# A mixture-of-experts decoder layer: the low halves of x1 made by VectorE, its scaling folded into a later addition, and the router stage in another order

## The chip, the cores and the metric

The kernel runs on one core of a Trainium2 chip. The metric is the device time of one execution in microseconds. A core has five engines, each with its own in-order instruction queue: TensorE (PE; PEld is its weight load), VectorE (DVE), ScalarE (ACT), GpSimd (POOL) and SyncE (SP), which here only starts transfers. An instruction waits on semaphores for results of other engines, and everything behind it in the same queue waits too.

## What is computed

One decoder layer on 512 tokens of 1024 numbers, all in float32. Two mixers work on a common projection of x: four mLSTM heads and eight attention heads with a sliding window. Then:

```python
y = concat(mlstm_out, att_out) @ w_out          # 512x1024 @ 1024x1024
x = layer_norm(ALPHA * x + y, ln1_w, ln1_b)     # "x1" in the kernel
# router: best of 4 groups, then the best 2 of that group's 8 experts
g_idx = argmax(x @ w_group_router + b_group_router)
top_v, top_i = top_k((x @ w_expert_router + b_expert_router)[group g_idx], 2)
out = sum over the 32 experts e of combine[:, e] * (silu(x @ w_gate[e]) * (x @ w_up[e])) @ w_down[e]
x = layer_norm(ALPHA * x + out, ln2_w, ln2_b)
```

An expert has three matrices of 1 MB, so the weights of the 32 experts are 96 MB.

## The kernel before, in words

The tokens are cut into four chunks of 128 rows; chunk c of x1 is one tile of 128x1024 (in the order listings the four tiles are x_2218, x_2221, x_2224 and x_2227, for chunks 0 to 3). The program has three parts.

The first part (up to about 200 us) is the projection and the two mixers. The second is the **router stage**, which the change rewrites. It is written out by hand: the order of the calls in the source is the order of the instructions on PE, DVE, ACT and POOL. For each chunk it has these steps:

- `out_mm`, `ml_late` (helper lines 194 to 196): the output projection on PE into the PSUM tiles `py`; three matmuls per product, since each operand is split in a high and a low half.
- `norm_a` (L864 to L867, then L199 and L200 on POOL): ALPHA * x + y and its statistics on DVE, then the reciprocal root on POOL.
- `norm_b` (L876, L877 on DVE; or L880 on POOL, L881 on ACT, L882 and L883): scale and shift, by halves of 512 columns. The table `NB` says which engine does which half. For chunk 2 it is DVE for half 0, and ACT and POOL for half 1; for chunk 3 it is DVE for both.
- `route_t`, `route_m` (L911, L912, L922): x1 is transposed on PE, copied from PSUM by ACT (`x1T`), and multiplied with the router's weights on PE into `lg`.
- `rd` (L931 to L954): the best group and the best two experts, some nine small instructions on DVE, ending in the one-hot tile `ohs` (L950). `rr` (L979 to L992): each token's rank inside its expert, by one to four small matmuls on `ohs` and five small DVE instructions, ending in `cola`.
- `x1_hi`, `x1_lo` (L895, L899): ACT makes a rounded copy `x1h` of x1 and another engine makes `x1l` = x1 - x1h. Both write column q*8+j of x1 to place (j, q), so x1 is read with a step of eight numbers, 32 bytes, and the copies are written in a row.
- `first_hot` (L1000, L1002): a one-hot matrix from `cola`, on DVE. `first_pick` (L1007): PE multiplies it with `x1h` and `x1l`, which gathers the tokens of the first two pairs of experts into four PSUM tiles `xp`. Per chunk these are 16 matmuls, four for each tile. A tile is complete when all four chunks are in it, and ACT then copies it (L1015).

When the last pick is done, the first pass through expert weights starts (`gu_part`, L1094). DVE meanwhile works out which expert takes which place (`slots_a`, L1198 to L1219), and PE and DVE turn that into the table `eid` (L1225).

The third part goes through 13 pairs of experts. SP loads weights in the order of use into a ring of buffers: seven of 8 KB per partition from the start, two more from another pool, five when the projection's weights are done with, four when `ml_late` is. The first six experts have fixed places and are loaded before the router is done; all others need `eid`, from which SP reads the expert's number, and a buffer that a pass has set free. Near the end `y_gather` (L1150, L1152) fetches each token's two expert results with eight gathers and adds them to x1 on DVE. Before that, x1 is multiplied by ALPHA, on POOL, right after the router stage (L1508).

Of the kernel before, what the change touches and what calls it, by code (L numbers as in the profile page):

```python
# [17 lines left out]
OP = mybir.AluOpType  # L18
# [5 lines left out]
NCH = 4  # L24
# [11 lines left out]
ALPHA = 2.0 ** 0.25  # L36
# [43 lines left out]
def layer_kernel(ctx, tc, x, w_in, conv_w, conv_b, gate_bias, norm_w, sinks, w_out, ln1_w, ln1_b,  # L80
# [17 lines left out]
    def close_pool(key):  # L98
        pools.pop(key)[0].__exit__(None, None, None)
# [7 lines left out]
    def open_ring(key, n, side):  # L107
        open_pool(key, n, 2 * DM, side)
        free.extend([key] * n)
# [514 lines left out]
    def prefetch(n):  # L624
        while loads and free and n > 0:
            p, i, b = loads.pop(0)
            if free[0] == "mix":
                key, ts = free.pop(0), [slot("we")[:, :DM] for _ in range(2)]
            else:
                t, key = rslot("we", n=2 * DM)  # L630
                ts = [t]
            assert key != "mix" or i == 2
            KEYS[p][i == 2].append(key)
            pairs[p][b][i] = load_part(ts, expert(SEATS[p][b]), i)
            n -= 1
# [234 lines left out]
    def norm_b(c, h):  # L870
        xc_ = x1[c]
        mv = n1[c][1]
        hs = slice(h * 512, (h + 1) * 512)
        xh_ = xc_[:, hs]
        if NB[c][h] == "V":
            V.scalar_tensor_tensor(xh_, xh_, mv[:, 0:1], l1w[:, hs], op0=OP.subtract, op1=OP.mult)  # L876
            V.scalar_tensor_tensor(xh_, xh_, mv[:, 2:3], l1b[:, hs], op0=OP.mult, op1=OP.add)  # L877
        else:
            if h == 0 or NB[c][0] == "V":
                G.tensor_scalar(mv[:, 3:4], mv[:, 2:3], mv[:, 0:1], -1.0, op0=OP.mult, op1=OP.mult)  # L880
            A.activation(xh_, xh_, AF.Identity, bias=mv[:, 3:4], scale=mv[:, 2:3])  # L881
            (V if NB[c][h] == "M" else G).tensor_mul(xh_, xh_, l1w[:, hs])  # L882
            G.tensor_add(xh_, xh_, l1b[:, hs])  # L883
# [9 lines left out]
    def x1_hi(c, halves=None):  # L893
        for hi, _, v in x1_parts(c, halves):
            A.activation(hi, v, AF.Copy)  # L895

    def x1_lo(c, halves=None, eng=G):
        for hi, lo, v in x1_parts(c, halves):
            eng.tensor_tensor(lo, v, hi, op=OP.subtract)  # L899

# [245 lines left out]
    def y_gather():  # L1146
        for c in range(NCH):
            for k in range(2):
                t = slot("yg")[:, :DM]
                G.indirect_dma_start(out=t, out_offset=None, in_=yd[:, :],  # L1150
                                     in_offset=bass.IndirectOffsetOnAxis(ap=yrow[:, 2 * c + k:2 * c + k + 1], axis=0))
                V.tensor_add(x1[c], x1[c], t)  # L1152

    def y_slots():
        return [slot(n, F32R)[:, :DM] for n in ("yh", "yl")]
# [205 lines left out]
    def rd(c, n):  # L1361
        if c not in gd:
            gd[c] = route_d(c)
        some(gd[c], n)
# [6 lines left out]
    with tc.manual_schedule(engines=MAN):  # L1371
        out_mm(0, 0, (0,), (0, 1))
        out_mm(0, 0, (1,), (0, 1))
        out_mm(0, 0, (0,), (2, 3))
        out_mm(0, 0, (1,), (2, 3))
        norm_a(0, (0,))
        norm_a(0, (1,))
        norm_b(0, 0)
        out_mm(1, 0, (0,), (0, 1))
        out_mm(1, 0, (1,), (0, 1))  # L1380
        out_mm(3, 1, (0,), (0, 1))
        norm_b(0, 1)
        out_mm(1, 0, (0,), (2, 3))
        out_mm(1, 0, (1,), (2, 3))
        route_t(0, (0,))
        out_mm(3, 1, (1,), (0, 1))
        route_m(0, (0,))
        route_t(0, (1,))
        out_mm(3, 1, (0,), (2, 3))
        route_m(0, (1,))  # L1390
        out_mm(2, 0, (0,), (0, 1))
        norm_a(1, (0,))
        norm_a(1, (1,))
        norm_b(1, 0)
        out_mm(3, 1, (1,), (2, 3))
        rd(0, 4)
        norm_b(1, 1)
        rd(0, 4)
        rd(0, 9)
        rr(0, 1)  # L1400
        x1_hi(0)
        route_t(1, (0,))
        x1_hi(1)
        close_pool("wr"); open_ring("ring1", NR // 2, "left"); prefetch(NR // 2); xs = xs_tiles()
        out_mm(2, 0, (0,), (2, 3))
        route_t(1, (1,))
        route_m(1, (0,))
        x1_lo(0)
        rr(0, 9)
        route_m(1, (1,))  # L1410
        out_mm(2, 0, (1,), (0, 1))
        par(first_hot(0))
        norm_a(2, (0,))
        rd(1, 4)
        first_pick(0, (0,))
        rd(1, 4)
        rr(1, 1)
        out_mm(2, 0, (1,), (2, 3))
        x1_lo(1)
        ml_late(3, ((0, 0), (1, 0)))  # L1420
        rd(1, 9)
        rr(1, 9)
        ml_late(3, ((2, 0), (3, 0)))
        par(first_hot(1))
        ml_late(3, ((0, 1), (1, 1)))
        ml_late(3, ((2, 1), (3, 1)))
        first_pick(0, (1,))
        norm_a(2, (1,))
        norm_b(2, 0)
        first_pick(1, (0,))  # L1430
        norm_a(3, (0,))
        norm_b(2, 1)
        first_pick(0, (2,))
        norm_a(3, (1,))
        route_t(2, (0,))
        route_t(2, (1,))
        norm_b(3, 0)
        route_m(2, (0,))
        norm_b(3, 1)
        route_m(2, (1,))  # L1440
        x1_hi(2)
        rd(2, 4)
        route_t(3, (0,))
        rd(2, 4)
        route_t(3, (1,))
        route_m(3, (0,))
        rr(2, 1)
        route_m(3, (1,))
        rd(2, 9)
        x1_hi(3, (0,))  # L1450
        first_pick(1, (2,))
        x1_lo(2)
        x1_hi(3, (1,))
        first_pick(0, (3,))
        first_pick(1, (1,))
        rr(2, 9)
        x1_lo(3, (1,), G)
        rd(3, 4)
        first_pick(1, (3,))
        rd(3, 4)  # L1460
        par(first_hot(2))
        rr(3, 1)
        first_pick(2, (3,))
        first_pick(2, (2,))
        slots_n()
        rd(3, 9)
        first_pick(2, (1,))
        x1_lo(3, (0,), G)
        rr(3, 9)
        first_pick(2, (0,))  # L1470
        par(first_hot(3))
        first_pick(3, (0, 1))
        par(slots_a())
        for g in range(2):
            pick_out(xs, xp0[g], g, eng=A)
        first_pick(3, (2, 3))
        for g in range(2, 4):
            pick_out(xs, xp0[g], g, eng=A)
        slots_e()
        pgs = [bank("pg")]  # L1480
        gu_part(pgs[0], xs, 0, pairs[0], TILES[ORDER[0]], 0)
        px = slots_b1()
        gu_part(pgs[0], xs, 0, pairs[0], TILES[ORDER[0]], 1)
        slots_b2(px)
        gu_part(pgs[0], xs, 0, pairs[0], TILES[ORDER[0]], 2)
        gu_part(pgs[0], xs, 0, pairs[0], TILES[ORDER[0]], 3)
# [7 lines left out]
    with tc.manual_schedule(engines={ENG.PE}):  # L1494
# [9 lines left out]
        ht = dn_t(h)  # L1504
        slots_c()
        pys.append(pass_dn(ht, 1))
    for c in range(NCH):
        G.tensor_scalar(x1[c], x1[c], ALPHA, None, op0=OP.mult)  # L1508
    for n, t in (("eid", eid), ("cwt", cwt), ("idf", idf), ("rank", rank)):
        show(n, t)  # L1510

# [272 lines left out]
```

## Time and profile before

| | us |
|---|---|
| median of three runs | 543.07 (540.05 to 543.82) |
| profiled execution | 538.57 |
| its span, first to last instruction | 536.7 |
| PE busy | 472.7 (88%) |
| DVE busy | 260.8 (49%) |
| ACT busy | 163.1 (30%) |
| POOL busy | 152.4 (28%) |

The span is the time from the first to the last instruction of the profiled execution; 1.9 us of its time lie outside. Busy shares are means over parts of the program with different limits, so they do not tell by themselves what bounds it. The chain of waits of this trace breaks off after the last 1.7 us, so what bounds each part is read from the slices, the timelines and the waits.

### The profile page before, as it was taken

The numbers are of one execution on the slowest core, as the hardware profiler recorded it, in microseconds if no ns is written. First come the engines' busy times: TensorE is split into PE (matmuls) and PEld (weight loads), VectorE is DVE, ScalarE is ACT, GpSimd is POOL, SyncE is SP. The second block draws the span as 40 slices with busy tenths as digits, with TensorE's granted clock in tenths as the row PEclk, the third lists the DMA queues.
The fourth block names the chain that finished last, engine by engine and source line by source line (L and its number), as shares of the span: only waits on it lengthen the run. The fifth ranks groups of instructions, "written<-read, shape, count | busy, mean of one in ns | idle before, by whom it ended". The sixth has DMA issues, their size and how long they took to land. (4 is left out here: it accounts for less than half of the span.)

```text
span 536.7 us, 8111 instructions
## 1 busy us (share of the span) xinstructions
PE 472.7 (88%) x2904; PEld 315.7 (59%) x2904; DVE 260.8 (49%) x589; ACT 163.1 (30%) x352; POOL 152.4 (28%) x178
## 2 busy tenths in 40 slices
PE   6999899999999999977899999999687996628990
PEld 5999688879899987766735633426112631324420
DVE  3453678884278675688973110303000300144883
ACT  3553545786444322414311111211110111000430
POOL 5479903422120111645821100000000001311451
PEclk9899979999999999999699999999977998757896
DMA  8624212220983539197559999999999999999504
GB/s 231 205 80 122 76 40 78 79 79 8 349 312 96 183 116 280 43 357 255 216 187 394 406 419 406 403 422 395 379 421 422 419 419 422 422 416 423 234 19 159
DMA packets 44907, 139.43 MB, mean 260 GB/s; under 512 B 6386, under 2 KB 17674, under 8 KB 41024
## 3 DMA queue, kind: packets, MB, share of 16 engines
q1 hardware_dynamic: 40944, 126.05, 62.7%
q0 software_dynamic: 3920, 12.84, 6.3%
q8 instruction: 24, 0.39, 0.3%
q14 instruction: 19, 0.16, 0.1%
HBM read 128.68 MB, written 10.49 MB: 259 GB/s over the span
## 5 line engine op out<-in xcount | busy, mean ns | idle before, releaser
L1094 PE MATMUL pg<-we,xs 128*32 128x512 f32 (+1 forms) x608 | 114.0, 645 | 16.1 <-DMA we<-in_w_exp_up 16.1
L1094 PEld LDWEIGHTS pg<-we,xs 128*32 128x32 f32 (+1 forms) x608 | 29.0, 127 | 86.9 <-issue 74.0
L245 PE MATMUL pj<-wh,xh 128*128 128x256 f32 (+1 forms) x224 | 63.8, 287 | 0.6 <-ACT wh L190 0.6
L246 PE MATMUL pj<-wh,xl 128*128 128x256 f32 (+1 forms) x224 | 62.8, 282 | 0.3 <-DVE xl L191 0.3
L1007 PE MATMUL xp<-ohr,x1h 128*128 128x256 f32 (+1 forms) x160 | 45.0, 314 | 18.3 <-ACT xs L1015 8.8
L250 PE MATMUL pj<-wl,xh 128*128 128x256 f32 x192 | 52.5, 279 | 0.0
L1143 POOL DMA_DIRECT2D yd<-y x11 | 6.1, 557 | 158.1 <-ACT y L1142 158.1
L1117 DVE COPY ht<-ph 128x256 f32<-128x256 f32 x13 | 5.5, 423 | 91.9 <-PE ph L1115 91.9
L1125 PE MATMUL yo<-we,ht 128*32 128x512 f32 (+1 forms) x304 | 47.4, 595 | 2.4 <-DVE ht L1117 1.8
L1007 PEld LDWEIGHTS xp<-ohr,x1h 128*128 128x128 f32 x160 | 34.6, 217 | 22.9 <-ACT xs L1015 8.9
L1007 PE MATMUL xp<-ohr,x1l 128*128 128x256 f32 (+1 forms) x160 | 44.1, 309 | 0.0
L245 PEld LDWEIGHTS pj<-wh,xh 128*128 128x128 f32 x224 | 42.4, 189 | 0.9 <-ACT wh L190 0.8
L246 PEld LDWEIGHTS pj<-wh,xl 128*128 128x128 f32 x224 | 42.4, 189 | 0.6 <-DVE xl L191 0.6
L1107 ACT ACTIVATE hid<-pg 128x256 f32<-128x256 f32 x13 | 5.0, 385 | 122.8 <-PE pg L1094 122.8
L250 PEld LDWEIGHTS pj<-wl,xh 128*128 128x128 f32 x192 | 35.6, 188 | 0.0
L1007 PEld LDWEIGHTS xp<-ohr,x1l 128*128 128x128 f32 x160 | 35.0, 219 | 0.0
L191 DVE TENSOR_TENSOR wl<-wraw,wh 128x1024 fp32r<-128x1024 f32 x14 | 21.2, 1528 | 23.0 <-ACT wh L190 22.9
L1125 PEld LDWEIGHTS yo<-we,ht 128*32 128x32 f32 (+1 forms) x304 | 14.4, 119 | 29.2 <-issue 24.4
L190 ACT ACTIVATE wh<-wraw 128x1024 fp32r<-128x1024 f32 (+2 forms) x23 | 23.2, 1021 | 12.3 <-DMA wraw<-in_w_in 3.5
L194 PE MATMUL pj<-xh,wh 128*128 128x512 f32 x64 | 26.7, 417 | 0.0
L196 PE MATMUL pj<-xl,wh 128*128 128x512 f32 x64 | 26.5, 414 | 0.0
L195 PE MATMUL pj<-xh,wl 128*128 128x512 f32 x64 | 26.3, 411 | 0.0
(363 smaller groups left out, 908.2 us busy)
## 6 DMA issues: line engine op xcount, KB each, us to landing
we<-in_w_exp_gate SPq DMA_DIRECT2D x64, 512.0 KB, 11.8
we<-in_w_exp_up SPq DMA_DIRECT2D x64, 512.0 KB, 12.2
we<-in_w_exp_down SPq DMA_DIRECT2D x30, 1024.0 KB, 13.5
wraw<-in_w_in SPq DMA_DIRECT2D x20, 512.0 KB, 3.7
yd<-y POOLq DMA_DIRECT2D x11, 512.0 KB, 7.6
xc<-in_x SPq DMA_DIRECT2D x4, 512.0 KB, 10.0
wo<-in_w_out SPq DMA_DIRECT2D x8, 256.0 KB, 5.0
wo<-in_w_out SPq DMA_DIRECT2D x4, 512.0 KB, 3.6
```

The lines of the kernel that those rows point to most:

```text
L190: A.activation(hi, src, AF.Copy)
L191: eng.tensor_tensor(lo, src, hi, op=OP.subtract)
L194: TE.matmul(o, lh, rh, start=start, stop=False)
L195: TE.matmul(o, ll, rh, start=False, stop=False)
L196: TE.matmul(o, lh, rl, start=False, stop=stop)
L245: TE.matmul(o, xh[j // 2][:, j % 2, cs], ws[i][j][0], start=j == 0, stop=False)
L246: TE.matmul(o, xl[j // 2][:, j % 2, cs], ws[i][j][0], start=False, stop=False)
L250: TE.matmul(o, xh[k // 2][:, k % 2, cs], ws[i][k][1], start=False, stop=k == 7)
L1007: TE.matmul(p_[:, j2, 0:P * n], w[c][:, 2 * g + j2], o[:, c, 0:P * n], start=c == 0 and s == 0 and j2 == 0, stop=c == NCH - 1 and s == 1 a ...
L1094: TE.matmul(pg[s:s + n], xs[k // 4][:, k % 4, P * b + s:P * b + s + n], ws[e][k // 4][:, :, k % 4], start=k == 0, stop=k == 7)
L1125: TE.matmul(py[u][s:s + n], ht[:, j, s:s + n], wt[e][2][j][:, 512 * u:512 * u + 512], start=j == 0, stop=j == 1)
L1143: G.dma_start(yd[p * P:(p + 1) * P], y)
```

## The change

Three things change. `x1_lo` runs on DVE for all four chunks and no longer on POOL. The four multiplications by ALPHA on POOL are gone; instead the first of the two additions to each chunk in `y_gather` is one `scalar_tensor_tensor`, x1 * ALPHA + t. And the router stage's calls stand in another order: the remaining output projection of chunks 2 and 3 comes ahead of the transposes of chunk 1, chunk 3's statistics come ahead of chunk 2's second scale-and-shift, the picks are made chunk by chunk, and chunk 3's halves of `x1_hi` and `x1_lo` are each one instruction.

```diff
-    def x1_lo(c, halves=None, eng=G):
+    def x1_lo(c, halves=None, eng=V):
...
-                V.tensor_add(x1[c], x1[c], t)
+                if k:
+                    V.tensor_add(x1[c], x1[c], t)
+                else:
+                    V.scalar_tensor_tensor(x1[c], x1[c], ALPHA, t, op0=OP.mult, op1=OP.add)
...
+        out_mm(2, 0, (0,), (2, 3))
...
+        x1_hi(0)
+        out_mm(2, 0, (1,), (0, 1))
         rr(0, 1)
...
+        x1_lo(0)
+        rr(0, 9)
+        out_mm(2, 0, (1,), (2, 3))
+        norm_a(2, (0,))
+        ml_late(3, ((0, 0), (1, 0)))
+        ml_late(3, ((2, 0), (3, 0)))
+        par(first_hot(0))
+        norm_a(2, (1,))
+        ml_late(3, ((0, 1), (1, 1)))
+        ml_late(3, ((2, 1), (3, 1)))
+        norm_a(3, (0,))
+        norm_b(2, 0)
+        x1_hi(1)
+        norm_a(3, (1,))
+        norm_b(2, 1)
         route_t(1, (0,))
...
+        x1_lo(1)
+        first_pick(0, (0, 1))
+        norm_b(3, 0)
         rd(1, 4)
...
+        norm_b(3, 1)
         first_pick(0, (2,))
...
-    for c in range(NCH):
-        G.tensor_scalar(x1[c], x1[c], ALPHA, None, op0=OP.mult)
```

The queue of POOL in the router stage, before (from the last scale-and-shift of chunk 1 on; `lnmv` is the tile with a chunk's statistics, here first chunk 2's and then chunk 3's):

```order
L883 TENSOR_TENSOR x_2221<-x_2221,l1b 128x512
L899 TENSOR_TENSOR x1l<-x_2218,x1h 128x1024
L899 TENSOR_TENSOR x1l<-x_2221,x1h 128x1024
L199 TENSOR_SCALAR lnmv<-lnmv 128x1
L200 TENSOR_TENSOR lnmv<-lnmv,mhalf 128x1
L880 TENSOR_SCALAR lnmv<-lnmv 128x1
L882 TENSOR_TENSOR x_2224<-x_2224,l1w 128x512
L883 TENSOR_TENSOR x_2224<-x_2224,l1b 128x512
L199 TENSOR_SCALAR lnmv<-lnmv 128x1
L200 TENSOR_TENSOR lnmv<-lnmv,mhalf 128x1
L899 TENSOR_TENSOR x1l<-x_2224,x1h 128x1024
```

and in the change:

```order
L883 TENSOR_TENSOR x_2221<-x_2221,l1b 128x512
L199 TENSOR_SCALAR lnmv<-lnmv 128x1
L200 TENSOR_TENSOR lnmv<-lnmv,mhalf 128x1
L199 TENSOR_SCALAR lnmv<-lnmv 128x1
L200 TENSOR_TENSOR lnmv<-lnmv,mhalf 128x1
L880 TENSOR_SCALAR lnmv<-lnmv 128x1
L882 TENSOR_TENSOR x_2224<-x_2224,l1w 128x512
L883 TENSOR_TENSOR x_2224<-x_2224,l1b 128x512
L1143 DMA yd<-y 128x1024
```

The low halves and the scalings have gone, and chunk 3's reciprocal root (the second L199 and L200) now stands ahead of chunk 2's L880.

The queue of ACT at the same place (- before, + the change; L881 is chunk 2's scale-and-shift, the L912 are the copies of transposed x1):

```order
 L895 ACTIVATE x1h<-x_2218 128x1024
-L912 COPY x1T<-rt 128x512
 L895 ACTIVATE x1h<-x_2221 128x1024
-L912 COPY x1T<-rt 128x512
-L954 COPY gls<-lg 128x4
 L881 ACTIVATE x_2224<-x_2224,lnmv 128x512
 L912 COPY x1T<-rt 128x512 x2
+L954 COPY gls<-lg 128x4
+L912 COPY x1T<-rt 128x512 x2
 L895 ACTIVATE x1h<-x_2224 128x1024
```

Before, chunk 1's two copies stand ahead of L881; in the change the first two L912 behind L881 are chunk 1's.

The queue of DVE in the change, from chunk 3's second statistics on:

```order
L864 SCALAR_TENSOR_TENSOR x_2227<-x_2227,py 128x512
L865 BN_STATS lnst<-x_2227 128x6
L867 BN_AGGR lnmv<-lnst 128x2
L899 TENSOR_TENSOR x1l<-x_2221,x1h 128x1024
L876 SCALAR_TENSOR_TENSOR x_2227<-x_2227,lnmv,l1w 128x512
L877 SCALAR_TENSOR_TENSOR x_2227<-x_2227,lnmv,l1b 128x512
L931 MAX gms<-lg 128x8
L933 MAX_INDEX gi<-gms,lg 128x8
L936 TENSOR_TENSOR ohg<-iot,gi 128x4
L939 SCALAR_TENSOR_TENSOR lg<-ohg,lg 128x32
L876 SCALAR_TENSOR_TENSOR x_2227<-x_2227,lnmv,l1w 128x512
L877 SCALAR_TENSOR_TENSOR x_2227<-x_2227,lnmv,l1b 128x512
```

Chunk 1's low half now stands between chunk 3's statistics and its scale-and-shift, and the search for chunk 1's best group (L931 on) between chunk 3's two halves. Before, chunk 1 was routed ahead of chunk 3's statistics.

## Rows read from the trace of the kernel before

**Rows 1.** the page's 40 slices of 13.4 us: busy tenths of the DMA engines

```profile
DMA  8624212220983539197559999999999999999504
```

**Rows 2.** SP's waits: line, releaser: us in total, times, longest

```profile
SPq L618 <- DVE eid L1225: 18.0, 1, 18.0
```

**Rows 3.** timeline of SP around the stage: start us, us, what

```profile
272.83 0.36 SPq L597 DMA_DIRECT2D we<-in_w_exp_gate  x1
```

**Rows 4.** timeline of PE in the stage

```profile
224.92 0.39 PE L195 MATMUL py<-woh,ams 128*128 128x512 f32 x1
225.15 0.40 PE L196 MATMUL py<-wol,ams 128*128 128x512 f32 x1
...
243.68 0.28 PE L1007 MATMUL xp<-ohr,x1h 128*128 128x256 f32 x1
243.80 0.28 PE L1007 MATMUL xp<-ohr,x1l 128*128 128x256 f32 x1
...
267.47 0.41 PE L1007 MATMUL xp<-ohr,x1h 128*128 128x256 f32 x1
267.68 0.41 PE L1007 MATMUL xp<-ohr,x1l 128*128 128x256 f32 x1
...
268.21 2.24 PE L1094 MATMUL pg<-we,xs 128*64 128x512 f32 x8
```

**Rows 5.** timeline of POOL in the stage

```profile
226.59 3.00 POOL L899 TENSOR_TENSOR x1l<-x,x1h 128x1024 fp32r<-128x1024 f32 x1
...
249.69 2.85 POOL L899 TENSOR_TENSOR x1l<-x,x1h 128x1024 fp32r<-128x1024 f32 x1 [2.13 <-ACT x1h L895]
...
259.90 11.23 POOL L1508 TENSOR_SCALAR x<-x 128x1024 f32<-128x1024 f32 x4
```

**Rows 6.** timeline of DVE in the stage; in brackets the idle time before

```profile
230.31 3.07 DVE L1002 SCALAR_TENSOR_TENSOR ohr<-iot,cola,ohr 128x256 fp32r<-128x256 f32 x1
...
234.63 0.16 DVE L931 MAX8 gms<-lg 128x8 f32<-128x8 f32 x1
...
238.16 0.48 DVE L1002 SCALAR_TENSOR_TENSOR ohr<-iot,cola,ohr 128x256 fp32r<-128x256 f32 x1
...
240.32 0.75 DVE L876 SCALAR_TENSOR_TENSOR x<-x,lnmv,l1w 128x512 f32<-128x512 f32 x1
...
242.50 0.68 DVE L864 SCALAR_TENSOR_TENSOR x<-x,py 128x512 f32<-128x512 f32 x1
...
245.33 0.21 DVE L867 BATCH_NORM_AGGREGATE lnmv<-lnst 128x2 f32<-128x12 f32 x1
...
250.20 2.37 DVE L936 TENSOR_TENSOR ohg<-iot,gi 128x4 f32<-128x4 f32 x1
```

**Rows 7.** groups by form: count, busy us, mean ns, idle before

```profile
L191 DVE TENSOR_TENSOR wol<-wo,woh 128x1024 fp32r<-128x1024 f32 x8 | 9.5, 1215 | 0.0
...
L190 ACT ACTIVATE woh<-wo 128x1024 fp32r<-128x1024 f32 x8 | 8.0, 1056 | 2.1 <-DMA wo<-in_w_out 2.1
...
L895 ACT ACTIVATE x1h<-x 128x1024 fp32r<-128x1024 f32 x3 | 6.5, 2156 | 0.0
...
L899 POOL TENSOR_TENSOR x1l<-x,x1h 128x1024 fp32r<-128x1024 f32 x3 | 8.9, 2957 | 2.7 <-ACT x1h L895 2.6
...
L912 ACT COPY x1T<-rt 128x512 f32<-128x512 f32 x8 | 4.7, 585 | 9.2 <-PE rt L911 9.1
```

**Rows 8.** timeline of ACT: chunk 2's second scale-and-shift

```profile
242.76 0.82 ACT L881 ACTIVATE x<-x,lnmv 128x512 f32<-128x512 f32 x1 [5.55 <-POOL lnmv L880]
```

**Rows 9.** windows of 1 us: PE busy, granted clock, DMA share, GB/s

```profile
408.00:409.00 1.00, 1.00 (x4) 0.50 1.02 418
...
412.00:413.00 1.00, 1.00 (x8) 0.88 1.00 418
...
467.00:468.00 1.00, 0.00 (x0) 0.50 1.01 418
```

**Rows 10.** group by line: the additions of the gathered results

```profile
L1152 DVE TENSOR_TENSOR x<-x,yg 128x1024 f32<-128x1024 f32 x8 | 9.8, 1226 | 33.4 <-DMA yg<-yd,yrow 33.4
```

More of the change, by code (lines that the diff above doesn't have):

```diff
@@ L1397, in layer_kernel @@
         norm_b(1, 1)
+        out_mm(2, 0, (0,), (2, 3))
         rd(0, 4)
-        rd(0, 9)
+        rd(0, 19)
+        x1_hi(0)
+        out_mm(2, 0, (1,), (0, 1))
         rr(0, 1)
-        x1_hi(0)
+        close_pool("wr"); open_ring("ring1", NR // 2, "left"); prefetch(NR // 2); xs = xs_tiles()
+        x1_lo(0)
[5 more added lines that the diff above has]
+        par(first_hot(0))
@@ L1402, in layer_kernel @@
+        norm_a(2, (1,))
[6 more added lines that the diff above has]
+        norm_b(2, 1)
         route_t(1, (0,))
-        x1_hi(1)
-        close_pool("wr"); open_ring("ring1", NR // 2, "left"); prefetch(NR // 2); xs = xs_tiles()
-        out_mm(2, 0, (0,), (2, 3))
         route_t(1, (1,))
         route_m(1, (0,))
-        x1_lo(0)
-        rr(0, 9)
         route_m(1, (1,))
-        out_mm(2, 0, (1,), (0, 1))
@@ L1412, in layer_kernel @@
-        par(first_hot(0))
-        norm_a(2, (0,))
+        x1_lo(1)
+        first_pick(0, (0, 1))
+        norm_b(3, 0)
         rd(1, 4)
[L1415 to L1432, printed above, removed]
+        norm_b(3, 1)
         first_pick(0, (2,))
-        norm_a(3, (1,))
+        rd(1, 19)
         route_t(2, (0,))
         route_t(2, (1,))
-        norm_b(3, 0)
+        rr(1, 9)
+        first_pick(0, (3,))
         route_m(2, (0,))
-        norm_b(3, 1)
         route_m(2, (1,))
         x1_hi(2)
-        rd(2, 4)
         route_t(3, (0,))
-        rd(2, 4)
+        par(first_hot(1))
@@ L1445, in layer_kernel @@
         route_t(3, (1,))
+        first_pick(1, (0, 1))
         route_m(3, (0,))
+        rd(2, 19)
+        route_m(3, (1,))
+        x1_hi(3)
         rr(2, 1)
[L1448 to L1451, printed above, removed]
-        x1_lo(2)
[L1453 to L1460, printed above, removed]
-        par(first_hot(2))
-        rr(3, 1)
@@ L1463, in layer_kernel @@
[L1463 to L1468, printed above, removed]
+        first_pick(1, (2, 3))
+        rd(3, 19)
+        rr(3, 1)
+        slots_n()
+        rr(2, 9)
+        x1_lo(2)
+        par(first_hot(2))
+        first_pick(2)
         rr(3, 9)
-        first_pick(2, (0,))
+        x1_lo(3)
         par(first_hot(3))
```

## The prediction

> **What bounds the kernel now.** I read the page's slices first, then the waits of SP, then the timelines of the four compute engines through the router stage, and last the groups by form for the prices.
>
> In the slices [rows 1] the reader is to see two stretches. From the 22nd slice (282 us) to the 37th the DMA engines are nine tenths busy or more: the weights stream in, and nothing done by an engine there shortens the run. In the two slices before it (255 to 282 us) they are half busy. They stand idle because all 18 buffers are full with the weights of the first six experts, and the next load needs two things from the router stage: the expert's number and a buffer that the first pass has set free. SP waits 18.0 us for `eid` [rows 2] and issues the first such load at 272.83 [rows 3], 4.6 us after the first pass has begun on PE at 268.21; that pass begins right behind the last pick, issued at 267.68 [rows 4]. So the last pick of the router stage is what counts: a microsecond there is a microsecond at the end.
>
> Inside the stage DVE and POOL get in each other's way. While POOL makes a low half (226.59 and 249.69, about 3 us each [rows 5]) a DVE instruction with two inputs in SBUF stands: L1002 takes 3.07 us at 230.31, and 0.48 us at 238.16; L936 takes 2.37 us at 250.20 [rows 6] for an input of four columns. The multiplications by ALPHA, 11.23 us from 259.90 [rows 5], lie on the same stretch.
>
> **The change part by part.**
>
> *ALPHA.* Four POOL instructions go, four of the eight DVE additions become multiply-adds of the same 1024 columns. DVE waits 33.4 us for the gathers there [rows 10], so an extra 0.1 us each has cover; without it this would cost 0.4 us. What is saved on POOL is worth only the DVE time that it no longer blocks, which the sum below leaves out of DVE's list.
>
> *Low halves on DVE: price L.* No row shows DVE reading with a step of 32 bytes. Below: 1.22 us, DVE's own 1024 columns read in a row. Above: 2.96 us, POOL's price for this very instruction. Nearest is ACT, which reads the same x1 with the same step for `x1h`: 2.16 us against 1.06 in a row [all rows 7]. Twice 1.22 would be 2.4; its rate per column, 2.1 ns, gives 2.2. I take **L = 2.3 us**.
>
> The Trainium skill (Vector Engine (DVE) Microarchitecture Reference, section 5.2, Measured stream behaviour on trn2) gives 1.73 ns per column where one source hops at every element, and 2.50 where streams step by 24 words. An estimate from these is 1.85 and 2.64 us for L; by the line below the last pick would come at 267.9 or 271.1, and no run here shows either.
>
> *The order.* All of the output projection comes first: 42 matmuls at 0.23 us behind the one issued at 225.15 end at 235.4, where now the last of them is issued just ahead of the pick at 243.68 [rows 4]. What follows on PE then waits. Chunk 1's transposes are done by 236, but ACT's copies of them stand behind chunk 2's L881; that waits for POOL's L880, which now stands behind chunk 3's reciprocal root; that waits for chunk 3's statistics at the end of a long DVE list; and DVE goes from these straight into a low half that blocks POOL. PE has nothing to do for some 9 us.
>
> *The sum*, as the time of the last pick, in absolute times of this trace:
>
> 1. 12 matmuls from 225.4 give 228.2; rank matmul and product bring DVE to chunk 0's low half at 228.6. Ends 228.6 + L.
> 2. DVE's list up to chunk 3's aggregate: four add-and-statistics pairs (two take 242.50 to 245.33, so 5.7), two aggregates at 0.2, one scale-and-shift pair (2 x 0.75), rank and one-hot work 1.4 [rows 6]: 9.0.
> 3. Chunk 1's low half: L. POOL cannot start on chunk 3's root before it ends.
> 4. Root, L880, L881: now, for chunk 2 alone, 240.32 to 242.76 and 0.82 [rows 6, 8], 3.3 in all. Then one copy, 0.6 [rows 7], and nine logit matmuls at PE's half clock, which issues one in 0.21 us where the full clock issues one in 0.12 [rows 4], with the drain 2.2. Together 6.1, and DVE idle for the last 3 of them: it waits for the logits, and chunk 3's second scale-and-shift is queued behind that wait.
> 5. Chunk 1 from MAX to one-hot, 4.0 (234.63 to 238.64 [rows 6]), with 1.5 of scale-and-shift in it: 5.5.
> 6. Chunks 2 and 3, MAX to one-hot, 8.0, and their two low halves: 2L.
> 7. 16 picks of chunk 3, the last issued 0.1 + 15 x 0.21 = 3.3 later at half clock.
>
> Sum: 228.6 + 9.0 + 6.1 + 5.5 + 8.0 + 3.3 + 4L = 260.5 + 4L. With 2.3 that is 269.7, **2.0 us later** than 267.68. The stalls that POOL caused are gone, and four low halves and the new wait cost a little more than they did. At the full clock in steps 4 and 7 it is 258.1 + 4L.
>
> Why half clock: PE is at 0.50, its lower level of 1.2 GHz, in the window at 467 us, in which it does nothing; it is also at 0.50 in the window at 408, where it is busy again, and comes back only within the one at 412 [rows 9]. Nine idle microseconds in the change are longer, and a gap of two or more before the last picks comes again while DVE makes chunk 2's low half; now too the last picks run at half clock [rows 4].
>
> The loads into the last four buffers, which wait for `ml_late`, start about 8 us sooner and land in a stretch where nobody waits for them. The stores of x1 and the order of SP's queue do not change. The copies and SP's read of `eid` behind the last pick keep their length.
>
> The profiled execution took 538.57 us, 1.87 of it outside its span, and lies 4.5 below the median of the runs, 543.07. The sum is made against the profiled one, 538.57 + 2.0 = 540.6; carried over to the median it is **545.1**.
>
> **The rivals.**
>
> *Slower: the clock stays down.* If PE does not come back to full clock between its idle stretch and the last picks, the transposes and logits of chunks 2 and 3 and the nine picks queued between them, 43 matmuls on which DVE waits, take 0.09 us more each, 3.9 in all. The last pick comes 5.9 late, 549.0 us. For it: at 412 PE had been busy since 408 before the clock rose, and here short waits on ACT and DVE lie in between. Against it: picks, transposes and logits make a nearly closed stretch of 5 us behind step 4. It decides if the granted clock is 0.5 up to 256 us. The same end is reached at full clock before and L near 3.
>
> *Faster: DVE reads the step for nothing.* Then L is 1.22 and the last pick comes at 265.4 (half clock, 2.3 early, 540.8) or at 263.0 (full clock, 4.7 early, 538.4). For it: POOL, at 2.96 against more than two for rows in a line, hardly feels the step. Against it: ACT doubles. It decides if L899 takes under 1.5 us.
>
> *No change:* the stage's end moves and the run does not follow, because something else in the 268 us behind it evens it out: 543.1. The full slices [rows 1] speak against it.
>
> **How the numbers follow.** Forecast (L from 1.8 to 2.7, mixed clock, 0.0 to +3.6 us): 0.50. Clock down, or L near 3: 0.26. L small: 0.17, of which 0.05 beyond 1% with some gain that I do not see. No change: 0.07. The bound of 1%, 5.4 us, is about what a measurement of this kernel tells from no change; it holds the forecast, nearly all of the faster rival and the last case. So faster 0.06, the same 0.68, slower 0.26. The range goes from the best bound, 538.4, to a little above the slower rival, 549.5; L = 2.96 at half clock, 272.3 and so 547.7, lies inside.
>
> **What would show it.** L899 on DVE, four times, near 2.3 us (step 1 to 3, 6). PE idle from about 236 to 246 with ACT's L912 waiting for L881 (step 4). L931 of chunk 1 near 248, the last L1002 of the stage near 266, the last pick near 269.7, the first load behind `eid` near 275. No DVE instruction of a few columns over 1 us. The prediction is wrong if chunk 1's copies do not wait for L881, if L is near 1.2 or the clock stays down, or if the end does not follow the last pick.

## The result and the profile after

The changed kernel took 546.65 us (median of 8 runs, 545.94 to 553.86) against 541.77 for the kernel before (8 runs, 538.34 to 543.82): a ratio of 1.0118, 95% interval 1.007 to 1.0166. Run again beside other kernels it took 549.92 against 541.08, 1.0138 (1.0074 to 1.0203). So it is slower by 1.2 to 1.4%, 6 to 8 us by the ratios; the medians differ by 4.9 and 8.8. Ratios leave disturbed runs out, five of the 12 for the order alone below, so there the difference of the medians over all runs is given beside the ratio.

The profiled execution of the changed kernel has a span of 545.2 us, that of before 536.7. To set the router stage of the two against each other I count from one instruction that both have ahead of everything that was moved: VectorE's copy of chunk 0's expert numbers (L952, `idf`), at 226.48 before and 221.97 after. The changed kernel's run came there 4.5 us sooner by luck: by windows of 4 us, TensorE had been at half clock for 10 us in the program ahead of the stage before, and for none after. So 4.5 is to be added to times of after when they are held against those of before.

The slices of the page, after; each 13.6 us:

```profile
PEclk9999999999999999965599999999978999757896
DMA  8633213204936554694049999999999999999313
```

Against [rows 1] the DMA engines' 19th to 21st slices read 4, 0, 4 in place of 7, 5, 5, and the clock reads 6, 5, 5 in the 18th to 20th (232 to 273 us). SP's first load behind `eid`, which was at 272.83 [rows 3]:

```profile
279.00 0.36 SPq L597 DMA_DIRECT2D we<-in_w_exp_gate  x1
```

and PE's timeline in the stage of the changed kernel, to be set against [rows 4] (in brackets the idle time before an instruction, and what ended it):

```profile
230.72 1.04 PE L911 MATMUL rt<-ident,x 128*128 128x128 f32 x8
240.08 0.64 PE L920 MATMUL lg<-rb,triu 1*128 1x40 f32 x2 [8.32 <-ACT x1T L912]
240.65 3.63 PE L922 MATMUL lg<-rsc,x1T 128*128 128x40 f32 x16
...
268.67 0.58 PE L1007 MATMUL xp<-ohr,x1h 128*128 128x256 f32 x1 [2.91 <-DVE ohr L1002]
...
274.34 0.28 PE L1007 MATMUL xp<-ohr,x1l 128*128 128x256 f32 x1
```

From `idf` to the last pick the stage took 274.34 - 221.97 = 52.4 us, before 267.68 - 226.48 = 41.2: **11.2 us longer**. From the last pick to the first load it is 4.7 us after and 5.2 before, so the end of the stage sets the load as it did.

Where the time lies is seen in the first rows. PE has finished chunk 1's transposes and stands for 8.32 us until ACT has copied them. ACT's list at that place:

```profile
238.74 0.81 ACT L881 ACTIVATE x<-x,lnmv 128x512 f32<-128x512 f32 x1 [14.45 <-POOL lnmv L880]
239.46 1.05 ACT L912 COPY x1T<-rt 128x512 f32<-128x512 f32 x2
```

and POOL's, which ACT waits for:

```profile
234.94 1.80 POOL L199 TENSOR_SCALAR lnmv<-lnmv 128x1 f32<-128x1 f32 x1 [3.50 <-DVE lnmv L867]
236.82 0.97 POOL L200 TENSOR_TENSOR lnmv<-lnmv,mhalf 128x1 f32<-128x1 f32 x1
237.89 0.82 POOL L880 TENSOR_SCALAR lnmv<-lnmv 128x1 f32<-128x1 f32 x1
```

The copies take half a microsecond each and have been ready to go since 231.8; they stand behind L881, which waits for L880, which stands behind chunk 3's root (L199, L200). The windows of 1 us show what PE's clock did meanwhile (PE busy, PEld, DVE, ACT, POOL, granted clock, DMA share, GB/s):

```profile
230.00:231.00 1.00, 1.00 (x7) 0.79 (x6) 0.97 (x3) 0.00 (x0) 0.35 (x2) 1.00 0.98 410
235.00:236.00 1.00, 0.00 (x0) 0.00 (x0) 1.00 (x1) 0.00 (x0) 1.00 (x1) 0.71 1.03 418
236.00:237.00 1.00, 0.00 (x0) 0.00 (x0) 1.00 (x2) 0.00 (x0) 0.92 (x2) 0.50 1.04 426
271.00:272.00 1.00, 1.00 (x6) 1.00 (x6) 0.96 (x5) 0.00 (x0) 0.00 (x0) 0.50 0.00 0
273.00:274.00 1.00, 1.00 (x11) 1.00 (x11) 0.80 (x5) 0.75 (x2) 0.00 (x0) 1.00 0.00 0
```

It fell while PE stood, and stayed at 0.50, the lower level of 1.2 GHz, from 236 to 272, though PE was busy for 27.6 of these 36 us. VectorE was busy for 17.4 of them; before, it was busy for 5.1 of each 6 us in the stage. Now it waits for PE again and again:

```profile
244.32 0.17 DVE L931 MAX8 gms<-lg 128x8 f32<-128x8 f32 x1 [5.75 <-PE lg L922]
244.81 0.16 DVE L936 TENSOR_TENSOR ohg<-iot,gi 128x4 f32<-128x4 f32 x1
249.86 0.22 DVE L983 TENSOR_TENSOR rkt<-rsc,lg 128x64 f32<-128x64 f32 x1 [2.25 <-PE lg L981]
254.97 0.17 DVE L931 MAX8 gms<-lg 128x8 f32<-128x8 f32 x1 [3.25 <-PE lg L922]
262.71 0.22 DVE L983 TENSOR_TENSOR rkt<-rsc,lg 128x64 f32<-128x64 f32 x1 [5.78 <-PE lg L981]
...
265.85 1.99 DVE L899 TENSOR_TENSOR x1l<-x,x1h 128x1024 fp32r<-128x1024 f32 x1
...
269.13 2.03 DVE L899 TENSOR_TENSOR x1l<-x,x1h 128x1024 fp32r<-128x1024 f32 x1
...
271.46 0.48 DVE L1002 SCALAR_TENSOR_TENSOR ohr<-iot,cola,ohr 128x256 fp32r<-128x256 f32 x1
```

That is 17.0 us of waiting in the 24.1 from 238.57 to 262.71; the last three rows are two low halves and the end of the last one-hot matrix. The low halves as a group, and the additions with and without ALPHA, by groups of the whole program (busy us, mean ns of one):

```profile
L899 DVE TENSOR_TENSOR x1l<-x,x1h 128x1024 fp32r<-128x1024 f32 x4 | 8.2, 2046 | 0.0
...
L1155 DVE SCALAR_TENSOR_TENSOR x<-x,yg 128x1024 f32<-128x1024 f32 x4 | 4.9, 1226 | 27.4 <-DMA yg<-yd,yrow 27.4
L1153 DVE TENSOR_TENSOR x<-x,yg 128x1024 f32<-128x1024 f32 x4 | 4.9, 1225 | 6.5 <-DMA yg<-yd,yrow 6.5
```

A low half is 2.05 us on VectorE, against 2.96 on POOL [rows 7]; the multiplication by ALPHA inside an addition costs 1 ns; and L936, which POOL held up for 2.37 us [rows 6], takes 0.16. So far the parts do what they were meant to.

### The profile page after: what moved, and what is told of

It is laid out like the page before. It is cut to its first block, busy times and chain, and to the rows that moved or that the text cites. A ratio compares the mean times of both kernels' runs of the same rounds, so it can differ in the third digit from the quotient of the medians.

```text
span 545.2 us, 8102 instructions
## 1 busy us (share of the span) xinstructions
PE 476.4 (87%) x2904; PEld 321.2 (59%) x2904; DVE 252.8 (46%) x593; ACT 162.5 (30%) x351; POOL 130.9 (24%) x169
## 5 line engine op out<-in xcount | busy, mean ns | idle before, releaser
L1007 PE MATMUL xp<-ohr,x1h 128*128 128x256 f32 (+1 forms) x160 | 46.6, 323 | 18.2 <-ACT xs L1015 8.7
L1007 PEld LDWEIGHTS xp<-ohr,x1h 128*128 128x128 f32 x160 | 36.0, 225 | 21.9 <-ACT xs L1015 8.9
L1007 PE MATMUL xp<-ohr,x1l 128*128 128x256 f32 (+1 forms) x160 | 45.2, 315 | 0.0
L1007 PEld LDWEIGHTS xp<-ohr,x1l 128*128 128x128 f32 x160 | 36.2, 227 | 0.0
## 6 DMA issues: line engine op xcount, KB each, us to landing
xc<-in_x SPq DMA_DIRECT2D x4, 512.0 KB, 10.1
```

The costliest lines, as they stand in the source:

```text
L1007: TE.matmul(p_[:, j2, 0:P * n], w[c][:, 2 * g + j2], o[:, c, 0:P * n], start=c == 0 and s == 0 and j2 == 0, stop=c == NCH - 1 and s == 1 a ...
```

## The experiments

**Theory A**: the new order costs the time, by chunk 1's copies behind ACT's late instruction and by the half clock that follows; the two small edits are harmless or a gain. **Rival B**: the low halves on VectorE cost it. **Rival C**: the multiplication in the addition. **Rival D**, within the order: the wait alone, with the half clock a mere sign of it.

The measurements in one table. Stage is the time from `idf` to the last pick in the one profiled run of each; half clock is worked out from windows of 1 us over the stage, each counting twice what its granted clock lacks of 1.

| kernel | median us | ratio to before | 95% interval | stage us | at half clock us |
|---|---|---|---|---|---|
| before | 541.77 | 1 | | 41.2 | 9 |
| changed | 546.65 | 1.0118 | 1.007 to 1.0166 | 52.4 | 38 |
| changed, again | 549.92 | 1.0138 | 1.0074 to 1.0203 | 50.5 | 34 |
| before + ALPHA | 539.16 | 0.9957 | 0.9916 to 0.9998 | 40.9 | 14 |
| before + low halves | 540.71 | 0.9989 | 0.9951 to 1.0027 | 43.2 | 24 |
| before + both | 539.99 | 0.9972 | 0.9931 to 1.0012 | 41.0 | 20 |
| order alone | 547.14 | 1.0066 | 1.0023 to 1.011 | 46.6 | 20 |
| changed + 33 matmuls | 544.46 | 1.0086 | 1.0047 to 1.0124 | 43.2 | 7 |
| changed + 33 + 24 matmuls | 543.39 | 1.005 | 0.9999 to 1.0101 | 42.4 | 3 |
| copies ahead | 544.44 | 1.0072 | 1.0033 to 1.0111 | 45.4 | 20 |
| copies ahead + 79 matmuls | 549.38 | 1.016 | 1.0114 to 1.0206 | 49.1 | 10 |
| copies and router step ahead | 539.36 | 0.9962 | 0.9928 to 0.9996 | 41.5 | 20 |
| before + both + 11 matmuls | 537.21 | 0.9946 | 0.991 to 0.9982 | 38.2 | 7 |
| before + both + 11 + 12 matmuls | 539.93 | 0.9982 | 0.9946 to 1.0018 | 38.6 | 3 |

Each ratio is to runs of the kernel before that were taken beside it, whose medians were 540.85 to 541.77 us. The single profiles scatter by some microseconds outside the stage: from the last pick to the end of the span they show 269.0 (before) to 273.8 us, and I draw nothing from that part.

### One part at a time

The multiplication by ALPHA alone, in the order of before:

```
-                V.tensor_add(x1[c], x1[c], t)
+                if k:
+                    V.tensor_add(x1[c], x1[c], t)
+                else:
+                    V.scalar_tensor_tensor(x1[c], x1[c], ALPHA, t, op0=OP.mult, op1=OP.add)
...
-    for c in range(NCH):
-        G.tensor_scalar(x1[c], x1[c], ALPHA, None, op0=OP.mult)
```

> The kernel before with one part of the change alone: POOL's four multiplications by ALPHA are gone, and the first addition to each chunk does the scaling in the same VectorE instruction. Theory A (the new order costs the time, the two small edits are harmless): 540 to 542 us, that is 0 to 2 us under the kernel before (541.77), because the end after the last pick was 1.9 us shorter in the changed kernel's profiled run (547.1 - 274.3 = 272.8 against 270.9 goes the other way in part, so no more than that is claimed). Rival C (the scaling in the addition is itself a cost): over 543 us.

Measured 539.16, 0.9957 (0.9916 to 0.9998). Rival C falls; the edit is a small gain if anything, its interval ends just under 1. The reason given above for a gain does not hold: the end behind the last pick is 1.9 us longer in the changed kernel's profile, not shorter (545.2 - 274.3 = 270.9 against 536.7 - 267.7 = 269.0).

The low halves alone:

```
-    def x1_lo(c, halves=None, eng=G):
+    def x1_lo(c, halves=None, eng=V):
...
-        x1_lo(3, (1,), G)
+        x1_lo(3, (1,), V)
...
-        x1_lo(3, (0,), G)
+        x1_lo(3, (0,), V)
```

> The kernel before, in its own order, with all four low halves made by VectorE instead of POOL, and nothing else. Theory A (the order costs the time): within 2 us of the kernel before, because each low half is 1.9 to 2.2 us on VectorE in the changed kernel's trace against 2.96 us on POOL, and the waits of VectorE for POOL's share of them go. Rival B (the low halves on VectorE cost the time: four of about 2.0 us on the list that ends last): 546 to 550 us.

Measured 540.71, 0.9989 (0.9951 to 1.0027). Rival B falls for the order of before: eight microseconds of low halves on VectorE cost nothing that can be measured there. What VectorE no longer loses beside POOL fits that: in this run's trace chunk 0's L1002 takes 0.48 us in place of 3.07 and chunk 2's L936 0.16 in place of 2.37. That this is the whole reason is not shown.

The order alone, that is the changed kernel with POOL's low halves and POOL's multiplications put back:

```
-    def x1_lo(c, halves=None, eng=V):
+    def x1_lo(c, halves=None, eng=G):
...
+    for c in range(NCH):
+        G.tensor_scalar(x1[c], x1[c], ALPHA, None, op0=OP.mult)
```

> The changed kernel with its two small edits taken back: its order of the router stage alone, the low halves on POOL and POOL's four multiplications by ALPHA as before. Theory A (the order costs the time): slower than the kernel before by at least as much as the change, 546 to 552 us, and the granted clock goes to 0.50 at about 236 us of the span and stays there for over 30 us. Rival B (the low halves cost it): 541 to 543 us.

Measured 547.14 (539.54 to 551.9 over 12 runs), 1.0066 (1.0023 to 1.011); by the medians over all runs it is 6.3 us more than the kernel before. The sign is theory A's; the size is A's by the medians and below it by the ratio. The wait is there, though shorter by 2.6 us:

```profile
243.27 0.65 PE L920 MATMUL lg<-rb,triu 1*128 1x40 f32 x2 [5.75 <-ACT x1T L912]
```

```profile
239.56 0.78 POOL L199 TENSOR_SCALAR lnmv<-lnmv 128x1 f32<-128x1 f32 x1 [3.53 <-DVE lnmv L867]
```

Chunk 1's logits start 243.27 - 227.71 = 15.6 us behind `idf`, against 18.1 in the changed kernel. From the start of chunk 3's root to ACT's L881 it is 2.4 us here (239.56 to 241.94), 3.8 there (234.94 to 238.74), where the root runs beside VectorE's low half and takes 1.80 in place of 0.78 us. So in the new order the low halves on VectorE do lengthen the wait, and the stage is 46.6 us here against 50.5 and 52.4. Whether they cost time in that order is not shown: by the medians the order alone is as slow as the changed kernel, by the ratios it lies between, with intervals that overlap.

A number of A missed: the clock was at 0.50 here from 240 to 249 and again from 264 to 273, and not for 30 us on end. In windows of 2 us:

```profile
242.00:244.00 2.00, 0.73 (x3) 0.65 (x3) 0.00 (x0) 1.71 (x3) 1.17 (x1) 0.50 1.00 401
250.00:252.00 2.00, 1.24 (x13) 1.01 (x12) 0.81 (x6) 0.66 (x2) 0.00 (x0) 1.00 0.99 410
```

Why it came back at 250 in this run and did not in the changed kernel is not settled.

Both small edits in the order of before:

```
-    def x1_lo(c, halves=None, eng=G):
+    def x1_lo(c, halves=None, eng=V):
...
+                    V.scalar_tensor_tensor(x1[c], x1[c], ALPHA, t, op0=OP.mult, op1=OP.add)
...
-        G.tensor_scalar(x1[c], x1[c], ALPHA, None, op0=OP.mult)
```

> The kernel before in its own order, with both small edits: the low halves on VectorE and the scaling by ALPHA in the first addition. Theory A, the two parts add up: ratios 0.9957 and 0.9989 give 0.9946, 537.5 to 540 us, under both kernels. Rival (both take load off POOL, and one of them alone already gives all there is): 0.996 to 1.000.

Measured 539.99, 0.9972 (0.9931 to 1.0012). The two do not add up beyond what the first gives alone; the rival's bracket held, but the intervals are too wide to call the difference.

### The changed kernel once more

> The changed kernel once more, unedited, on the chip of the next three, so that they can be set against it and a second profile shows whether TensorE's half clock of 37 us is there in every run. Theory A (order, wait and clock): 545 to 549 us, granted clock 0.50 from about 12 us after chunk 0's last router step on VectorE, for at least 10 us.

Measured 549.92, a little above the range. Its profile shows the same wait of 8.3 us, at the same distance from `idf` (244.68 - 226.56 = 18.1 us; 240.08 - 221.97 = 18.1 in the first), and half clock for 34 us of the stage, with a return to full speed from 252 to 255:

```profile
244.68 0.65 PE L920 MATMUL lg<-rb,triu 1*128 1x40 f32 x2 [8.31 <-ACT x1T L912]
```

```profile
238.00:240.00 2.00, 0.00 (x0) 0.00 (x0) 1.93 (x4) 0.00 (x0) 0.46 (x1) 0.59 1.04 426
252.00:254.00 2.00, 1.23 (x12) 1.00 (x11) 0.38 (x3) 0.85 (x2) 0.00 (x0) 0.99 1.02 418
256.00:258.00 2.00, 2.00 (x11) 2.00 (x12) 0.43 (x4) 0.30 (x1) 0.00 (x0) 0.50 0.03 8
```

This run came to the stage with as much half clock behind it as before's (`idf` at 226.56 and 226.48), so its stage of 50.5 us against 41.2 is the cleaner comparison: **9.3 us**.

### The clock without the wait

33 matmuls that nobody needs, in the 8.3 us in which PE stood:

```
+    def heat(n):
+        xp0.append(bank("xp", tag="m").rearrange("p (j n) -> p j n", j=2))
+        for i in range(n):
+            TE.matmul(xp0[0].rearrange("p j n -> p (j n)"), x1h[0][:, 0], x1h[0][:, 0:4], start=True, stop=True)
...
         route_t(1, (1,))
+        heat(33)
         route_m(1, (0,))
```

> The changed kernel with 33 further matmuls on TensorE, 128 x 512 from chunk 0's high half into a bank that the picks overwrite later; they stand between chunk 1's transposes and its logits, where TensorE was idle for 8.3 us, and take 33 x 0.233 = 7.7 us. They add work only, and no wait is taken away. Theory A in its form that the clock carries the loss: the granted clock stays at 1.00 over 236 us and for most of the stage, and the time falls by 5 to 9 us, to 538 to 542 us. Rival D (the wait for chunk 1's copies alone costs the time, the clock is a sign of it): the same as the changed kernel, 545.5 to 548 us.

Measured 544.46, 1.0086 (1.0047 to 1.0124): 2.2 and 5.5 us under the changed kernel's two medians, and still 3.6 over the kernel before. The wait is untouched, with the logits at 246.58 - 228.34 = 18.2 us behind `idf` as before; the granted clock stays at 1.00 until 263, and the stage is 43.2 us long in place of 50.5 and 52.4:

```profile
246.58 0.41 PE L920 MATMUL lg<-rb,triu 1*128 1x40 f32 x2 [0.91 <-ACT x1T L912]
246.92 1.98 PE L922 MATMUL lg<-rsc,x1T 128*128 128x40 f32 x16
```

```profile
258.00:260.00 2.00, 2.00 (x22) 2.00 (x22) 0.50 (x5) 0.81 (x1) 0.00 (x0) 1.00 0.06 25
264.00:266.00 2.00, 0.61 (x3) 0.61 (x4) 1.97 (x10) 0.00 (x0) 0.00 (x0) 0.50 0.00 0
```

So rival D falls in its strict form: 544.46 lies under the 545.5 to 548 that it gave, and 8 of the 12 runs lie below the lowest of the changed kernel's 13, 545.94. The intervals of the ratios overlap, though, so the size of the gain is not settled. Theory A was too generous to the clock: 544.46 lies above the 538 to 542 that it gave. The clock is a part of the loss, and the wait with PE at full speed is another: 3.6 us are left with 7 us of half clock in the stage, fewer than the 9 of before.

24 more matmuls ahead of chunk 2's picks, where the clock fell at 264:

```
+    def heat2(c, n):
+        for i in range(n):
+            TE.matmul(pls[c][:, 256:512], x1h[0][:, 0], x1h[0][:, 0:2], start=True, stop=True)
...
+        heat2(3, 24)
         first_pick(2)
```

> As the run with 33 added matmuls (544.46 us), with 24 more of 128 x 256 (24 x 0.12 = 2.9 us) ahead of chunk 2's picks, where TensorE waited 2.9 us for VectorE and the clock fell at 264 us. The granted clock should stay 1.00 through the whole stage. What is then left over the kernel before is the new order's waits alone: 542 to 544 us if the clock was 2 to 4 us of the loss and the waits 1 to 3; under 541 us if the clock was all of it; 544 to 547 if waits are all of it.

Measured 543.39, 1.005 (0.9999 to 1.0101). The clock fell at 262 all the same, though PE had been busy since 260, and the 24 took 4.37 us in place of 2.9; it was back at 1.00 at 266, and 3 us of half clock are left of 34 to 38:

```profile
260.00:262.00 2.00, 1.91 (x21) 1.88 (x21) 2.00 (x8) 0.00 (x0) 0.00 (x0) 0.94 0.04 8
262.00:264.00 2.00, 2.00 (x11) 2.00 (x11) 1.97 (x10) 0.00 (x0) 0.00 (x0) 0.50 0.00 0
```

What remains over the kernel before, 2.3 us, is what the order costs with the clock nearly out of it; its interval touches 1.

### The wait without the clock

ACT's, POOL's and VectorE's lists in another order, PE's untouched:

```
-        norm_a(3, (0,))
         norm_b(2, 0)
+        route_t(1, (0,))
+        route_t(1, (1,))
         x1_hi(1)
-        norm_a(3, (1,))
+        norm_a(3, (0,))
         norm_b(2, 1)
-        route_t(1, (0,))
-        route_t(1, (1,))
+        norm_a(3, (1,))
```

> The changed kernel with only the order on ScalarE, VectorE and POOL repaired, TensorE's order untouched: chunk 1's two copies of its transposes stand ahead of its high half and of chunk 2's normalization on ScalarE, and chunk 2's second half is normalized ahead of chunk 3's second half. If the copies' place behind chunk 3's root is what costs the time: chunk 1's logits start 5 to 8 us earlier against chunk 0's last router step, and the time is 541 to 544 us. Rival (VectorE's list, not the copies, sets the stage): 545 to 548 us, the same as the changed kernel.

Measured 544.44, 1.0072 (1.0033 to 1.0111), 0.4 us above the first reading's range and under the rival's. Chunk 1's logits start 233.40 - 223.30 = 10.1 us behind `idf`, 8 sooner. But PE stands again, ahead of chunk 2's transposes, for 6.78 us:

```profile
233.40 0.41 PE L920 MATMUL lg<-rb,triu 1*128 1x40 f32 x2 [0.29 <-ACT x1T L912]
...
244.44 1.09 PE L911 MATMUL rt<-ident,x 128*128 128x128 f32 x4 [6.78 <-ACT x1T L912]
```

and what holds up ACT is a copy of four columns, L954, which waits for chunk 1's router step on VectorE, and that step stands behind chunk 3's normalization there:

```profile
243.65 0.16 ACT L954 COPY gls<-lg 128x4 f32<-128x4 f32 x1 [7.14 <-DVE lg L939]
243.71 0.59 ACT L912 COPY x1T<-rt 128x512 f32<-128x512 f32 x1
```

One wait of the same kind has taken the place of the other: chunk 2's transposed copy behind something late on ACT. In the last run chunk 1's router step goes ahead of it:

```
         route_m(1, (1,))
+        rd(1, 19)
         x1_lo(1)
...
         norm_b(3, 0)
-        rd(1, 4)
         norm_b(3, 1)
         first_pick(0, (2,))
-        rd(1, 19)
```

> The run with the copies ahead (544.44 us) with one move more: chunk 1's router step on VectorE stands right behind its logits, ahead of chunk 1's low half and of chunk 3's normalization. In that run ScalarE's copy of the group logits, which waits for that router step, stood ahead of chunk 2's transposed copies and TensorE was idle for 6.8 us. If waits of this kind, ScalarE's list in order behind something late, are what the order costs: TensorE's idle time there falls to 2 to 4 us (until chunk 2's second half is normalized), and the time to 540.5 to 543 us. If VectorE's list sets the stage: chunk 3's normalization comes 2 us later instead, and it stays at 543.5 to 546 us.

Measured **539.36, 0.9962 (0.9928 to 0.9996)**, better than expected: under the changed kernel's medians by 7.3 and 10.6 us, and not slower than the kernel before. PE's long wait is down to 1.60 us, for chunk 2's normalization itself, and the copies follow at once:

```profile
242.48 0.66 PE L911 MATMUL rt<-ident,x 128*128 128x128 f32 x4 [1.60 <-POOL x L883]
```

```profile
241.40 0.16 ACT L954 COPY gls<-lg 128x4 f32<-128x4 f32 x1 [1.69 <-DVE lg L939]
241.46 0.59 ACT L912 COPY x1T<-rt 128x512 f32<-128x512 f32 x1
```

Its stage is 41.5 us though 20 us of it run at half clock. The output projection first, the low halves on VectorE and the folded ALPHA are all still in it, and it takes no longer than the order of before with the same two edits (539.99). With the two late instructions gone from ahead of ACT's copies the whole loss is back. The rows show that PE waited for these copies; but the moves put chunk 2's normalization and chunk 1's router step earlier on VectorE as well, and what each list gave is not separated.

Copies ahead and added matmuls together, in PE's new wait:

```
+        heat2(1, 55)    # into pls[1][:, 256:512]
         route_t(2, (0,))
...
+        heat2(3, 24)
         first_pick(2)
```

> The changed kernel with the copies ahead (544.44 us) and, besides, 55 added matmuls of 128 x 256 (55 x 0.12 = 6.5 us) in TensorE's idle 6.8 us ahead of chunk 2's transposes and 24 in the later wait for VectorE. It takes away chunk 1's wait and the half clock both. If these two are the whole loss: 540 to 542 us, the kernel before within 1 us. If another part of the order costs time as well (all eight output products ahead of chunk 1's router step, so that VectorE runs dry behind them): 542 to 544 us.

Measured 549.38: it tells nothing of either theory. The added matmuls wrote into the bank that the late L954 reads, waited for it in their turn, and then took 8.22 us of PE's time on the path:

```profile
247.13 8.22 PE L1084 MATMUL lg<-x1h 128*128 128x256 f32 x55 [6.63 <-ACT gls L954]
```

### Added matmuls in the order of before

With both small edits the order of before has a wait of 2.67 us on PE, after which the clock was at 0.50 for 20 us:

```profile
246.12 1.11 PE L911 MATMUL rt<-ident,x 128*128 128x128 f32 x4 [2.67 <-POOL x L883]
```

```
+        heat3(3, 11)    # as heat, into xp0[3]
         route_t(2, (1,))
```

> The kernel before in its own order with both small edits (539.99 us, 0.9972), and 11 matmuls more of 128 x 512 into chunk picks' fourth bank, in the 2.67 us in which TensorE waited for chunk 2's second half and after which its granted clock was 0.50 for 20 us. If half clock in that stretch costs time: the stage from chunk 0's last router step to the last pick falls from 41.3 us to 37 to 40, and the time to 535 to 539 us, a ratio of 0.988 to 0.996. If VectorE's list sets the stage whatever the clock: 539 to 541 us, 0.996 to 1.000.

Measured **537.21, 0.9946 (0.991 to 0.9982)**, the lowest median of the study, under both kernels. The stage is 38.2 us against 41.0 without the 11 matmuls, one profile each, and the window that read 0.50 reads 1.00 (first without, then with them):

```profile
246.00:248.00 2.00, 1.88 (x8) 1.47 (x8) 1.23 (x2) 0.73 (x2) 1.18 (x3) 0.50 0.88 320
```

```profile
246.00:248.00 2.00, 2.00 (x17) 1.79 (x17) 1.23 (x3) 1.44 (x2) 1.01 (x2) 1.00 0.96 354
```

The intervals of the two ratios overlap (0.991 to 0.9982 with them, 0.9931 to 1.0012 without), so the gain in the run's time is likely, 10 of 12 runs with them being below 10 of 11 without, but not settled.

Twelve more in a second place:

```
+        heat2(2, 12)
         rr(2, 1)
```

> As the run before this one with 12 further matmuls of 128 x 256 ahead of chunk 2's rank product, where the kernel before waited 1.92 us for VectorE and its clock fell behind it. If the clock there matters: 0 to 2 us under the run before this one. If TensorE was not idle there any more: the added 1.4 us show and it is 0 to 1.5 us slower than that run.

Measured 539.93, 0.9982 (0.9946 to 1.0018), above the run without them in the direction of the second reading, though by 2.7 us where it had 0 to 1.5. VectorE now waits 1.95 us for the product behind them where it waited 0.44 (with 12 more first, then without):

```profile
248.76 0.22 DVE L983 TENSOR_TENSOR rkt<-rsc,lg 128x64 f32<-128x64 f32 x1 [1.95 <-PE lg L981]
```

```profile
251.57 0.22 DVE L983 TENSOR_TENSOR rkt<-rsc,lg 128x64 f32<-128x64 f32 x1 [0.44 <-PE lg L981]
```

The stage is 0.4 us longer, and the two intervals overlap, so the 2.7 us are not shown to be a loss; between 537.21 and 539.36 too no difference is shown. What is shown is that each of these two, the 11 matmuls in the order of before and the two moves, is faster than the kernel before.

## Why the prediction was right, and where it was not

The time, 546.65, lies within the range and 1.5 us from the forecast, and the wait was the one described. But the case that came is not the likeliest. It is the rival with the clock that stays down, which together with L near 3 had a chance of 0.26: its condition, a granted clock of 0.5 up to 256 us, is met in the first profile (to 272), and in the second but for the return from 252 to 255.

By the steps of the sum, times of after plus 4.5:

- *Step 1*, chunk 0's low half from 228.6: 223.98 + 4.5 = 228.5. Right.
- *Step 2*, VectorE's list, 9.0: 8.6. Right.
- *L*, 2.3: 2.23, 1.94, 1.99 and 2.03. Right, a little high. The nearest row, ACT's step of 32 bytes at twice its time [rows 7], led well, and the rival with L = 1.22 is out. The Trainium skill's figures (Vector Engine (DVE) Microarchitecture Reference, section 5.2), by which L was estimated at 1.85 and 2.64, hold these four values between them.
- *Step 4*, from the low half's end to chunk 1's logits on VectorE, 6.1: 7.6. The chain of root, L880, L881 and copies came as written, PE idle and ACT's L912 behind L881. The logits were mis-sized. I counted nine matmuls at 0.21 us; a chunk's logits are 16 rows of L922 and two of L920, 4.2 us at half clock (240.08 to 244.28), and 2.3 at full clock in the run with the 33 matmuls.
- *Step 5*, 5.5: 7.4 (244.32 to the end of L1002 at 251.71), of which 2.25 is VectorE's wait for the product of L981 behind PE's slow list. I had put nothing there.
- *Step 6*, chunks 2 and 3, 8.0 + 2L = 12.6: 20.2. **This is the step that failed.** It took VectorE to be the one that sets the pace and left the logits of chunks 2 and 3 hidden. They were not: 3.25 and 5.78 us of waiting for PE, at half clock. In the run with the 33 matmuls, with the clock at 1.00 there, the same two waits are 0.89 and 2.26 us (rows below), so 5.9 of the 9.0 us come with the half clock, and 3.1 are the new order's with PE at full speed.
- *Step 7*, 3.3: 2.4, since the clock came back in the middle of the last picks, at 273.

The two waits of step 6 in the run with the 33 matmuls:

```profile
255.25 0.17 DVE L931 MAX8 gms<-lg 128x8 f32<-128x8 f32 x1 [0.89 <-PE lg L922]
...
259.46 0.22 DVE L983 TENSOR_TENSOR rkt<-rsc,lg 128x64 f32<-128x64 f32 x1 [2.26 <-PE lg L981]
```

Together the stage is 11.2 us longer, 9.3 in the second profile, where the forecast said 2.0 and the rival 5.9. The rival's price was too low, in part for the reason of step 4: it took 43 matmuls, and the logits among them count twice. The first load behind `eid`, forecast near 275, came at 279.0, in times of before 283.5.

The runs themselves are 6 to 8 us slower, not 9 to 11. The profiled run of before is a good one: 538.57 against a median of 541.77. It has 9 us of half clock in its stage, where the three kernels in the same order had 14 to 24; but their stages, 40.9 to 43.2 us, are little longer, so where its other microseconds come from stays open. That the forecast lies within 1.5 us is luck: it promised 2.0 of the 6 to 8, and it was built on the median of three runs, 543.07, which is 1.3 above the median of eight.

That ALPHA costs nothing, that VectorE is no longer blocked, and that the end follows the last pick came as forecast. What the prediction did not see is that the loss went with two instructions ahead of ACT's copies. It named the first, L881 behind chunk 3's root. The second, L954 ahead of chunk 2's copies, lies hidden behind the first and shows only when that is taken away.

What stays open: why the granted clock returned within 10 us in some runs with the same wait and did not in others; and whether the repaired order with added matmuls of its own would fall below 537 us, which was not tried in a form that worked.

## What to carry to other kernels

When a list is reordered so that one engine gets all its work early, look at what stands ahead of the small copies that feed it: an engine in order makes a copy of half a microsecond as late as the latest instruction before it, and here two such places, with the moves that mended them, were worth 7 to 11 us. After the first is mended, read the wait again, for another of the same kind may lie behind it. And price every step that a short idle stretch of TensorE may put at half clock by counting its rows in the trace, not its calls in the code.

## What the runs showed of the hardware

- VectorE's subtraction of two sources with 1024 columns, of which one is read with a step of 32 bytes, takes 1.94 to 2.25 us in these runs, and 2.72 with POOL's addition (L883) beside it (the run with the copies ahead, and that with 79 matmuls besides), against 1.22 in a row and 2.96 on POOL.
- What half clock costs depends on who waits for TensorE. In the order of before with both small edits the stage was 41.0 us with 20 us of it and 38.2 with 7; in the changed order, where VectorE waits for TensorE at each step, 50.5 and 52.4 with 34 and 38 us of it and 43.2 with 7.
- Matmuls without a use, put into a wait of TensorE, held its granted clock at 1.00 behind it: 2.8 us of them went with a stage of 38.2 us in place of 41.0, 7.8 us of them with 43.2 in place of 50.5 and 52.4. Put where the engine was not idle, 12 of 0.12 us showed as 1.5 us more of waiting on VectorE.
- The clock can fall while TensorE is busy, a little after an idle stretch: in the run with 33 and 24 matmuls TensorE was busy for 0.64 of the 2 us up to 260 and for 1.91 of the next 2, and it was at 0.50 from 262.
- It can also stay down while TensorE is busy: in the changed kernel the profile has TensorE busy for all of the 14 us from 250 to 264, with transposes, logits and picks behind each other, and the granted clock at 0.50 throughout.
